# A two-layer hybrid encoder on one core: one late tile in three outputs, softmax scalings on another engine, ten matmuls ahead of the first

## The chip, the cores and the metric

The kernel runs on one core of a Trainium2 chip. Its time is the device time of one execution in microseconds; three runs of the kernel before gave 2385.94, 2385.95 and 2386.65 us, median 2385.95. A core has five engines with queues of their own: PE (TensorE, matrix products into PSUM), DVE (VectorE), ACT (ScalarE), POOL (GpSimd) and SP (SyncE, which here issues every transfer). They are ordered among each other by semaphores alone.

## The reference

Two layers of the following, on `x` of 512 tokens by 1024 channels, in float32:

```python
x = x + 0.5 * swiglu(rmsnorm(x, ffn1_norm[l]), ffn1_w1[l], ffn1_w2[l])
h = rmsnorm(x, mix_norm[l])
q, k, v, xr, yr, gl = jnp.split(h @ w_in[l], SPLITS, axis=-1)
# 16 query heads, 4 key heads of 64: per-head rmsnorm, rotary, softmax over all 512 keys
attn = block_attention(q, k, v) @ w_attn_o[l]
# depthwise conv of xr, two gated linear recurrences (forward, backward), times gelu(yr)
rnn = (hr * jax.nn.gelu(yr)) @ w_rnn_o[l]
merged = gates[:, :, 0] * attn + gates[:, :, 1] * rnn      # sigmoid gates from gl
x = x + merged @ w_out[l]
x = x + 0.5 * swiglu(rmsnorm(x, ffn2_norm[l]), ffn2_w1[l], ffn2_w2[l])
```

## The kernel before

Activations lie channel-major: a tile is 128 channels by 512 tokens, and `x` is 8 such tiles. Every float32 product is made of three matmuls on PE (`mm3`, L233): operands are split in a high and a low part, and high x high, high x low and low x high are accumulated in PSUM. `run` (L238) makes one output tile of 128 channels from 8 (or 22, or 4) input tiles that way. Weights come as one ordered stream of chunks of four tiles; SP loads them nine chunks ahead, and ACT (`wh`) and DVE (`wl`) split them six chunks ahead.

The order of all other work is tied to the matmul stream. Behind every second input tile `run` calls `step()`. Work is queued with `later(n, fn)` and issued n steps on; what an engine gets in which order follows from that alone, and each engine works its queue strictly in that order.

A layer is: first FFN half; the mixing phase; second FFN half. In the mixing phase the input projections of the recurrent branch and of the gates run on PE, and the attention and the recurrence run beside them as side work. Attention is made in 64 units over both layers (a head and half of the queries, two tiles of 128 queries each). For a unit, PE makes the scores (`u_sc`, L635), DVE their row maxima (`u_max`, L639) and from both the negated, scaled bias for the exponential (L641), ACT the exponential `p` with row sums, DVE the reciprocal of the sums (L649) and that times 2^14 (L650), POOL the high half of the probabilities (`pH`, by L114), DVE their low half (by L108). Then they are transposed by a transfer, and PE multiplies them with the values (L684). The names `un` are the small tiles of a unit: maxima, bias, sums, reciprocals.

The recurrence uses `xc` (the convolution), `tr` and `ti` (its gates, and then its terms), `y` (the gelu). POOL has `ti` (L111) and one step of `y` (L114) of it.

At the end of the phase stand three projections: `rnn`; `aoa` and `ao` (the first and the second four input tiles of the attention's output projection); and `wo`, the output projection of the phase, whose eight input tiles are the merged tiles `mg`. Evacuating an output m of `ao` (`ev_ao`, L885) makes, on DVE, the attention's part `aa` and the gated `th`, adds the recurrent part (on POOL, for the last output on DVE), and then splits the sum into `mh` (ACT) and `ml` (DVE):

Of the kernel before, what the change touches and what calls it, by code (L numbers as in the profile page):

```python
# [9 lines left out]
F32R = mybir.dt.float32r  # L10
# [8 lines left out]
KD = D // 128  # L19
# [10 lines left out]

GELU_K = 0.7978845608028654

# k tiles per weight chunk, 2 KB slots of the pool, chunks loaded and split ahead
KC = 4

NT = 99
LOAD_AHEAD = 9
SPLIT_AHEAD = 6

# side work, in steps of six matmuls of the main stream: lags of its stages, where the  # L40
# gate chunks go, and heads started per step
PV_LAG = 6
N_LAGS = (4, 2)
G_LAGS = (1, 2, 3, 5, 7)
# [4 lines left out]
GATES_3 = 1  # L49
GATES_4 = 0  # L50
AO_AT = 4
Q1_AT = 0
RATES = {"kv": 0.0, "q": 0.33, "xr": 0.33, "gA": 0.33, "gB": 0.33, "yr": 0.33, "lru0": 0.3, "lru1": 0.3, "rnn": 0.6, "aoa": 0.6, "ao": 0.0, "wo": 0.0}

# [2 lines left out]
def tile_griffin_encoder(  # L57
# [55 lines left out]
    def gts(out, a, s1, s2, op0=ALU.mult, op1=ALU.mult):  # L113
        G.tensor_scalar(out=out, in0=a, scalar1=s1, scalar2=s2, op0=op0, op1=op1)  # L114
# [1 line left out]
    def f32(ap):  # L116
        return ap.bitcast(F32)

    # ---- steps: side work is queued against the progress of the main matmul stream
    pend = []  # L120
    clock = [0, 0]
    launcher = []
# [5 lines left out]
    def step():  # L128
        clock[0] += 1
        while pend and pend[0][0] <= clock[0]:  # L130
            heapq.heappop(pend)[2]()
        for f in launcher:
            f()
# [2 lines left out]
        while pend:  # L136
            step()

    # ---- weights: one ordered stream of chunks, loaded ahead and split ahead
    chunks = []  # L140

    KS = {"aoa": (0, KD // 2), "ao": (KD // 2, KD)}
# [81 lines left out]
    def next_w():  # L224
        i = pos[2]
        pos[2] += 1
        load_to(i + 1)
        split_to(i + 1)
        load_to(i + 1 + LOAD_AHEAD)
        split_to(i + 1 + SPLIT_AHEAD)  # L230
        return split.pop(i)

    def mm3(ps, wh, wl, xh, xl, start, stop):  # L233
        PE.matmul(ps, wh, xh, start=start, stop=False)  # L234
        PE.matmul(ps, wh, xl, start=False, stop=False)  # L235
        PE.matmul(ps, wl, xh, start=False, stop=stop)  # L236
# [8 lines left out]
            if k % 2 == 1:  # L245
                step()

    # ---- constants
    ones = const.tile([128, 128], F32R, name="ones")
    idn = const.tile([128, 128], F32, name="idn")  # L250
    tabs = const.tile([128, 2, 4, HD], F32, name="tabs")
# [10 lines left out]
        prm_t[l] = t  # L262

    class Norm:
        """h = x * gain in two parts per tile, and the sum of squares over the tiles."""

        def __init__(self, l, col):
            self.l, self.col = l, col
# [46 lines left out]
                V.tensor_reduce(out=rtok, in_=d3, op=ALU.add, axis=AX)  # L315
            return r, rtok

    # ---- SwiGLU half step: x += 0.5 * (silu(h @ w1g) * (h @ w1u)) @ w2
    def ffn(norm, on_x, during=None, r_at=0):
        h = norm.h  # L320
        at = [None] * KF
# [58 lines left out]
            else:  # L380
                fin()

    # ---- per-layer vectors for the mixing phase
    def layer_vectors(l):
        p = prm_t[l]
        v = {}
# [50 lines left out]
        v["tb"] = tb  # L437
        return v

    # ---- mixing phase  # L440
    def mix(l, norm, v, on_x):
        p = prm_t[l]
        hb, hc, nhc, sc, tb = v["hb"], v["hc"], v["nhc"], v["sc"], v["tb"]
# [26 lines left out]
        vs = {}  # L470
        ready = [0]

        # heads of q or k: per-head norm, rotary, two fp16 parts, transposed
        def heads(src, n, cs, stack_h, stack_l, dst_T):
            st = {}

# [131 lines left out]
            for t in range(4):  # L608
                later(8 + t, lambda t=t: v3(t))

        # attention: (pair of heads, half of the queries, head, query tile)
        units = [(pp, hf, hi) for pp in range(NH // 2) for hf in range(2) for hi in range(2)]
        attn = [None] * KD
        up = [0, 0.0, 0.0]
# [9 lines left out]
        def unit(pp, hf, hi):  # L624
            head, kv = 2 * pp + hi, pp // 2
            mx, nb, su, ri, rs = (sm("un", 2) for _ in range(5))
            ps, pe = [None, None], [None, None]
            src = []

            def u_sc(ti):  # L630
                ps[ti] = PS()
                q = qT[head // 8, 2 * hf + ti]
                for kt in range(4):
                    for j in range(2):
                        PE.matmul(ps[ti][:, kt * 128:(kt + 1) * 128], q[:, head % 8, :], kT[kt][:, 2 * kv + j, :],  # L635
                                  start=j == 0, stop=j == 1)

            def u_max(ti):
                V.tensor_reduce(out=mx[:, ti:ti + 1], in_=ps[ti], op=ALU.max, axis=AX)  # L639
                if ti == 1:  # L640
                    V.tensor_scalar(out=nb, in0=mx, scalar1=sc, scalar2=-1.0, op0=ALU.mult, op1=ALU.mult)  # L641

            def u_exp(ti):
                pe[ti] = T("p")
                act(pe[ti], ps[ti], ACTF.Exp, bias=nb[:, ti:ti + 1], scale=sc, accum_out=su[:, ti:ti + 1])

            def u_inv(ti):
                if ti == 0:
                    V.reciprocal(ri, su)  # L649
                    V.tensor_scalar(out=rs, in0=ri, scalar1=2.0 ** 14, scalar2=None, op0=ALU.mult)  # L650

            def u_hi(ti):
                if ti == 0:
                    src.extend(T("pH", F16, (128, 2, 512)) for _ in range(2))
                gts(src[0][:, ti], pe[ti], ri[:, ti:ti + 1], 2.0 ** 14)

            def u_lo(ti):
                stt(src[1][:, ti], pe[ti], rs[:, ti:ti + 1], src[0][:, ti], ALU.mult, ALU.subtract)

            def u_tr():  # L660
                dst = [T("PT", F16, (128, 2, 4, 128)) for _ in range(2)]
                for i in range(2):
                    SP.dma_start_transpose(dst[i].rearrange("p a b c -> p (a b) c"),
                                           src[i].rearrange("p a b -> p (a b)"))
                pts[pp, hf, hi] = dst

            u_sc(0)
            later(1, lambda: u_sc(1))
            for n, f in zip(U_LAGS, (u_max, u_exp, u_inv, u_hi, u_lo)):
                for ti in range(2):  # L670
                    later(n + ti, lambda f=f, ti=ti: f(ti))
            later(U_LAGS[5], u_tr)
            if hi == 1:
                later(U_LAGS[5] + PV_LAG, lambda: pv(pp, hf))
# [24 lines left out]

        launcher.append(launch)  # L700

        # q, k, v: token-major
        def qkv_chunk(ps, k, src):
            wh, wl = next_w()
            hh, hl = src[k]
# [28 lines left out]
                heads([q[:] for q in q_t], 8, tb["q"], stack_h(qview), stack_l(qview),  # L734
                      lambda t, s_: trans_q(i, t, s_))

        # recurrent branch
        rnn = [None] * KD
        rst = {}

# [115 lines left out]
            for n, f in zip(G_LAGS, (e1, e2, e3, e4, e5)):  # L856
                later(n, f)

        # gates and output projections
        th = {}  # L860
        tm = [None] * KD
        mg = [None] * KD
# [53 lines left out]
        for op, m in mix_ops:  # L916
            up[2] = RATES[op]
            if op[:3] == "lru":
                lru(m, int(op[3]))
                continue  # L920
            if op in ("kv", "q"):
                qkv(op, m)
                continue
            if m == 0 and op in ("rnn", "ao"):
                while pend and (rst if op == "rnn" else True):
                    if op == "ao":
                        up[2] = 1.0
                    step()
                for k in range(2):
                    fetch(1 if op == "rnn" else 0, k)  # L930
            if op == "ao" and m == 0:
                launcher.pop()
            if op == "wo" and m == 0:
                for k in range(KD):
                    x[k] = T("x")
                    SP.dma_start(out=x[k], in_=xsave[k])
            if op in ("rnn", "ao"):
                fetch(1 if op == "rnn" else 0, m + 2)
            ps = PS()
            run(ps, {"rnn": rnn, "aoa": attn, "ao": attn, "wo": mg}.get(op, hn), *KS.get(op, (0, KD)))  # L940
            if m == KD - 1 and op in ("ao", "wo"):
                evac[op](m, ps)
            else:
                later(1, lambda op=op, m=m, ps=ps: evac[op](m, ps))

    with tc.manual_schedule():
        V.memset(f32(ones), 1.0)
        V.memset(epsb, EPS)
        warm = const.tile([128, 1], F32, name="warm")
        act(warm, epsb, ACTF.Tanh)  # L950
        load_prm(0)
        for k in range(KD):
            x[k] = T("x")
        norm = Norm(0, P_G1)
        for k in range(KD):
            SP.dma_start(out=x[k], in_=xT[k])
            if k in (0, 3, 6):
                load_to(pos[0] + 1)
        load_to(5)
        for k in range(KD):  # L960
            norm.add_h(k)
            if k in (0, 3, 7):
                split_to(pos[1] + 1)
        split_to(4)
        for k in range(KD):
            later(1 + k, lambda k=k: norm.add_sq(k))
        later(18, norm.close)
        later(30, lambda: SP.dma_start(out=tabs, in_=rope))
        later(30, lambda: SP.dma_start(out=idn, in_=ident))

        for l in range(L):
            nmix = Norm(l, P_GM)
            vecs = {}
            ffn(norm, nmix.add, lambda: vecs.update(layer_vectors(l)), 0 if l else 2)
            nf = Norm(l, P_G2)
            if l + 1 < L:
                load_prm(l + 1)
            mix(l, nmix, vecs, nf.add)
            if l + 1 < L:
                norm = Norm(l + 1, P_G1)  # L980
                ffn(nf, norm.add)
            else:
                ffn(nf, lambda m: SP.dma_start(out=outT[m], in_=x[m]))
        drain()
# [68 lines left out]
```

## Time and profile before

| | |
|---|---|
| median of three runs | 2385.95 us |
| span of the profiled execution (first to last instruction) | 2385.1 us |
| mean granted TensorE clock, share of 2.4 GHz | 0.997 |
| PE busy | 2359.3 us, 99%, 11604 matmuls |
| DVE busy | 1519.6 us, 64% |
| ACT busy | 1035.8 us, 43% |
| POOL busy | 263.1 us, 11%, 236 instructions |
| chain that ended last | PE 90%, DVE 5%, ACT 3%, DMA 1% |

The profiled execution has no time of its own beside its span; the runs' median lies 0.85 us above the span. Busy time of PE is modelled and its matmuls overlap, so its share is not a measure of speed; what counts is when the next matmul starts and what it waited for. The busy shares are means over stages with different limits: DVE, 64% in the mean, is over 90% busy in those twelve of the forty equal slices of the span that hold the mixing phase's middle. An instruction's row shows its start in us from the first instruction, its length in us, and in brackets the idle time of its engine before it with what ended that.

### The profile page before, as it was taken

How to read it: one execution, taken by the hardware profiler on the slowest of the kernel's cores; microseconds unless marked ns; L12 is line 12 of the kernel's file. 1: busy time of each engine (PE TensorE's matmuls, PEld its weight loads, DVE VectorE, ACT ScalarE, POOL GpSimd, SP SyncE). 2: the span in 40 equal slices, each digit the busy share in tenths (PEclk: the TensorE clock that was granted, in tenths of full speed). 3: DMA queues.
4: the chain of work that ended last, by engine and by line, in shares of the span. 5: the costliest groups of instructions: out<-in, count | busy, mean ns of one | idle time of the engine just before them, and what ended most of it. 6: DMA issues, size and time to landing. Idle time of an engine off the chain costs nothing.

```text
span 2385.1 us, 31932 instructions
## 1 busy us (share of the span) xinstructions
PE 2359.3 (99%) x11604; PEld 1927.3 (81%) x11604; DVE 1519.6 (64%) x2520; ACT 1035.8 (43%) x1892; POOL 263.1 (11%) x236
## 2 busy tenths in 40 slices
PE   8999999999999999999999999999999999999999
PEld 7888888877778788888888888888787787888887
DVE  6555536899995755553355555378999966655521
ACT  5333324678863333232233333256788533333321
POOL 1000000122331200000000000001223312000000
PEclk9999999999999999999999999999999999999999
DMA  5222333676488232223332223336665972222331
GB/s 202 97 86 85 102 98 110 155 157 150 118 206 240 89 98 88 88 84 111 109 103 89 84 85 110 107 94 157 158 149 124 209 231 95 97 85 85 93 98 66
DMA packets 299486, 285.83 MB, mean 120 GB/s; under 512 B 175936, under 2 KB 184512, under 8 KB 299328
## 3 DMA queue, kind: packets, MB, share of 16 engines
q1 hardware_dynamic: 299328, 283.79, 42.4%
q8 instruction: 91, 1.49, 0.3%
q14 instruction: 67, 0.55, 0.1%
HBM read 229.18 MB, written 14.68 MB: 102 GB/s over the span
## 4 chain that ended last, share of the span: by engine, by line
PE 90%; DVE 5%; ACT 3%; DMA 1%; issue 1%; SPq 0%; DVEq 0%; ACTq 0%
PE ps L234 27%; PE ps L235 27%; PE ps L236 27%; PE ps L708 2%; PE ps L635 2%; PE ps L710 2%; PE ps L709 2%; PE ps L684 1%; DVE wl L105 1%; DVE pH L108 1%; DVE tr L108 0%; ACT p L102 0%; DVE un L639 0%; DMA x<-in_xT_dram 0%; ACT L102 0%
## 5 line engine op out<-in xcount | busy, mean ns | idle before, releaser
L105 DVE TENSOR_TENSOR wl<-wr,wh 128x512 fp32r<-128x512 f32 (+1 forms) x848 | 580.5, 717 | 69.9 <-ACT wh L102 68.5
L234 PE MATMUL ps<-hh,wh 128*128 128x512 f32 x1408 | 549.0, 390 | 6.2 <-ACT wh L102 5.7
L235 PE MATMUL ps<-hl,wh 128*128 128x512 f32 x1408 | 548.7, 390 | 0.2 <-DVE hl L108 0.2
L236 PE MATMUL ps<-hh,wl 128*128 128x512 f32 x1408 | 548.5, 390 | 0.0
L102 ACT ACTIVATE wh<-wr 128x512 fp32r<-128x512 f32 (+1 forms) x848 | 477.2, 602 | 80.4 <-DMA wr<-in_w2b_dram 68.5
L234 PEld LDWEIGHTS ps<-hh,wh 128*128 128x128 f32 x1408 | 264.8, 188 | 61.9 <-ACT wh L102 5.7
L235 PEld LDWEIGHTS ps<-hl,wh 128*128 128x128 f32 x1408 | 264.8, 188 | 56.3 <-DVE hl L108 1.3
L236 PEld LDWEIGHTS ps<-hh,wl 128*128 128x128 f32 x1408 | 264.7, 188 | 54.8 <-DVE wl L105 0.2
L234 PE MATMUL ps<-ah,wh 128*128 128x512 f32 x704 | 273.9, 389 | 0.0
L235 PE MATMUL ps<-al,wh 128*128 128x512 f32 x704 | 273.9, 389 | 0.0
L236 PE MATMUL ps<-ah,wl 128*128 128x512 f32 x704 | 273.9, 389 | 0.0
L102 ACT ACTIVATE ah<-u 128x512 fp32r<-128x512 f32 x88 | 55.7, 633 | 376.5 <-DVE u L105 376.5
L234 PE MATMUL ps<-hnh,wh 128*128 128x512 f32 x512 | 207.8, 406 | 6.6 <-ACT tr L102 5.4
L108 DVE SCALAR_TENSOR_TENSOR x<-ps,x 128x512 f32<-128x512 f32 x48 | 33.2, 691 | 271.3 <-PE ps L236 271.3
L236 PE MATMUL ps<-hnh,wl 128*128 128x512 f32 x512 | 201.0, 393 | 0.0
L235 PE MATMUL ps<-hnl,wh 128*128 128x512 f32 x512 | 200.2, 391 | 0.0
L111 POOL TENSOR_TENSOR sq<-sq,sq 128x512 f32<-128x512 f32 x42 | 56.7, 1350 | 1132.4 <-ACT sq L102 1118.3
L102 ACT ACTIVATE hh<-x,prm 128x512 fp32r<-128x512 f32 x48 | 34.5, 723 | 314.8 <-DVE x L108 310.4
L105 DVE TENSOR_TENSOR u<-ps,R 128x512 f32<-128x512 f32 x88 | 60.8, 691 | 168.7 <-PE ps L236 168.7
L102 ACT ACTIVATE th<-g 128x512 f32<-128x512 f32 x88 | 55.6, 632 | 245.7 <-DVE g L105 245.7
L114 POOL TENSOR_SCALAR pH<-p,un 128x512 f16<-128x512 f32 x128 | 115.6, 913 | 351.3 <-DVE un L649 197.9
L234 PEld LDWEIGHTS ps<-ah,wh 128*128 128x128 f32 x704 | 132.1, 188 | 27.5
(157 smaller groups left out, 3465.7 us busy)
## 6 DMA issues: line engine op xcount, KB each, us to landing
wr<-in_w1a_dram SPq DMA_DIRECT2D x176, 256.0 KB, 2.7
wr<-in_w1b_dram SPq DMA_DIRECT2D x176, 256.0 KB, 2.7
wr<-in_wfm_dram SPq DMA_DIRECT2D x128, 256.0 KB, 3.3
wr<-in_w2a_dram SPq DMA_DIRECT2D x80, 256.0 KB, 2.7
wr<-in_w2b_dram SPq DMA_DIRECT2D x80, 256.0 KB, 2.8
wr<-in_wqkv_dram SPq DMA_DIRECT2D x48, 256.0 KB, 2.9
gsave<-lg SPq DMA_DIRECT2D x32, 256.0 KB, 3.3
wr<-in_wro_dram SPq DMA_DIRECT2D x32, 256.0 KB, 3.9
```

Of the source, the lines that this page charges most:

```text
L102: A.activation(out, in_, func, **kw)
L105: V.tensor_tensor(out=out, in0=a, in1=b, op=op)
L108: V.scalar_tensor_tensor(out=out, in0=a, scalar=s, in1=b, op0=op0, op1=op1)
L111: G.tensor_tensor(out=out, in0=a, in1=b, op=op)
L114: G.tensor_scalar(out=out, in0=a, scalar1=s1, scalar2=s2, op0=op0, op1=op1)
L234: PE.matmul(ps, wh, xh, start=start, stop=False)
L235: PE.matmul(ps, wh, xl, start=False, stop=False)
L236: PE.matmul(ps, wl, xh, start=False, stop=stop)
L635: PE.matmul(ps[ti][:, kt * 128:(kt + 1) * 128], q[:, head % 8, :], kT[kt][:, 2 * kv + j, :], start=j == 0, stop=j == 1)
L708: PE.matmul(ps[t], hh[:, ts_], wh, start=k == 0, stop=False)
L709: PE.matmul(ps[t], hh[:, ts_], wl, start=False, stop=False)
L710: PE.matmul(ps[t], hl[:, ts_], wh, start=False, stop=k == KD - 1)
```

## The change

It has three parts.

- In `wo`, the first three outputs are made by a new function, `run_open`: it makes input tiles one to seven of the first output, then of the second, then of the third, leaving all three accumulations open in PSUM, and after that the eighth input tile of each of the three. Their evacuations are issued one, two and three steps later. The other five outputs are made by `run` as before.
- In a unit's softmax, DVE's maximum gives the negated maximum, and its scaling to the bias goes to POOL, one instruction for each query tile behind its maximum. The scaling of the reciprocal by 2^14 goes to POOL too, and the high half takes the scaled reciprocal.
- Ahead of everything, POOL sets a tile to ones and PE makes ten matmuls of it.

```diff
+    def run_open(pss, rhs, kl):
+        held = []
+        for ps in pss:
+            for k in range(kl):
+                if k % KC == 0:
+                    wh, wl = next_w()
+                sl = slice(k % KC * 128, (k % KC + 1) * 128)
+                mm3(ps, wh[:, sl], wl[:, sl], *rhs[k], k == 0, False)
+                if k % 2 == 1:
+                    step()
+            held.append((wh, wl))
+        sl = slice(kl % KC * 128, (kl % KC + 1) * 128)
+        for ps, (wh, wl) in zip(pss, held):
+            mm3(ps, wh[:, sl], wl[:, sl], *rhs[kl], False, True)
+            yield ps
...
             def u_max(ti):
-                V.tensor_reduce(out=mx[:, ti:ti + 1], in_=ps[ti], op=ALU.max, axis=AX)
-                if ti == 1:
-                    V.tensor_scalar(out=nb, in0=mx, scalar1=sc, scalar2=-1.0, op0=ALU.mult, op1=ALU.mult)
+                V.tensor_reduce(out=mx[:, ti:ti + 1], in_=ps[ti], op=ALU.max, axis=AX, negate=True)
+                gts(nb[:, ti:ti + 1], mx[:, ti:ti + 1], sc, 1.0)
...
                     V.reciprocal(ri, su)
-                    V.tensor_scalar(out=rs, in0=ri, scalar1=2.0 ** 14, scalar2=None, op0=ALU.mult)
+                    gts(rs, ri, 2.0 ** 14, 1.0)
...
-                gts(src[0][:, ti], pe[ti], ri[:, ti:ti + 1], 2.0 ** 14)
+                gts(src[0][:, ti], pe[ti], rs[:, ti:ti + 1], 1.0)
...
                     SP.dma_start(out=x[k], in_=xsave[k])
+                for i, ps in enumerate(run_open([PS() for _ in range(WO_OPEN)], mg, KD - 1)):
+                    later(1 + i, lambda m=i, ps=ps: evac["wo"](m, ps))
+                continue
+            if op == "wo" and m < WO_OPEN:
+                continue
...
+        idle = T("idle", F32R)
+        G.memset(f32(idle), 1.0)
+        pw = PS()
+        for _ in range(WARM):
+            PE.matmul(pw, idle[:, 0:128], idle, start=True, stop=True)
```

`WO_OPEN` is 3, `WARM` is 10, `gts` is a `tensor_scalar` on POOL. On the engines the change looks as follows; tile numbers differ between the two kernels, and line numbers by two.

PE in the first layer's `wo`, before: the end of the first output, with input tile seven (`mh_8147`) and input tile eight (`mh_8159`), and the begin of the second (`ps_8218`).

```order
L236 MATMUL ps_8179<-mh_8121,wl_8026 128x512
L234 MATMUL ps_8179<-mh_8147,wh_8025 128x512
L235 MATMUL ps_8179<-ml_8148,wh_8025 128x512
L236 MATMUL ps_8179<-mh_8147,wl_8026 128x512
L234 MATMUL ps_8179<-mh_8159,wh_8025 128x512
L235 MATMUL ps_8179<-ml_8160,wh_8025 128x512
L236 MATMUL ps_8179<-mh_8159,wl_8026 128x512
L234 MATMUL ps_8218<-mh_7984,wh_8053 128x512
L235 MATMUL ps_8218<-ml_7985,wh_8053 128x512
```

PE in the changed kernel at the same place: input tile seven is `mh_8192`, and behind it the second output (`ps_8225`) begins.

```order
L236 MATMUL ps_8224<-mh_8192,wh_8070 128x512
L237 MATMUL ps_8224<-ml_8193,wh_8070 128x512
L238 MATMUL ps_8224<-mh_8192,wl_8071 128x512
L236 MATMUL ps_8225<-mh_8029,wh_8098 128x512
L237 MATMUL ps_8225<-ml_8030,wh_8098 128x512
```

Farther on, at the end of the third output's seven tiles, input tile eight (`mh_8204`) comes for all three.

```order
L236 MATMUL ps_8226<-mh_8192,wh_8178 128x512
L237 MATMUL ps_8226<-ml_8193,wh_8178 128x512
L238 MATMUL ps_8226<-mh_8192,wl_8179 128x512
L236 MATMUL ps_8224<-mh_8204,wh_8070 128x512
L237 MATMUL ps_8224<-ml_8205,wh_8070 128x512
L238 MATMUL ps_8224<-mh_8204,wl_8071 128x512
L236 MATMUL ps_8225<-mh_8204,wh_8126 128x512
L237 MATMUL ps_8225<-ml_8205,wh_8126 128x512
L238 MATMUL ps_8225<-mh_8204,wl_8127 128x512
```

So the matmuls of input tile eight moved behind 42 others, and those of tile seven kept their place in the first output.

ACT at the end of the first layer's `ao`, before: the high halves of merged tiles six, eight (`mh_8159`) and seven (`mh_8147`), with weight splits between.

```order
L102 ACTIVATE mh_8121<-th_8020 128x512
L102 ACTIVATE mh_8159<-th_8076 128x512
L102 ACTIVATE wh_8182<-wr_8079 128x512
L102 ACTIVATE mh_8147<-th_8048 128x512
L102 ACTIVATE wh_8202<-wr_8105 128x512
```

ACT in the changed kernel at the same place, where tile eight is `mh_8204` and tile seven `mh_8192`.

```order
L104 ACTIVATE mh_8166<-th_8065 128x512
L104 ACTIVATE mh_8204<-th_8121 128x512
L104 ACTIVATE wh_8229<-wr_8124 128x512
L104 ACTIVATE mh_8192<-th_8093 128x512
L104 ACTIVATE wh_8249<-wr_8150 128x512
```

Nothing moved here.

POOL in the first layer's attention, before: one unit's two `pH` and the recurrence's `ti` and gelu's `y` around them.

```order
L111 TENSOR_TENSOR ti_5830<-ti_5830,tr_5828 128x512
L114 TENSOR_SCALAR pH_6086<-p_5954,un_5863 128x512
L114 TENSOR_SCALAR pH_6086<-p_5972,un_5863 128x512
L111 TENSOR_TENSOR ti_6021<-ti_6021,tr_6019 128x512
L114 TENSOR_SCALAR y_6142<-y_6142 128x512
L114 TENSOR_SCALAR pH_6204<-p_6122,un_5979 128x512
```

POOL in the changed kernel at the same place: `un` with `scs` is the scaling of a maximum to the bias, `un` from `un` alone that of the reciprocals.

```order
L113 TENSOR_TENSOR ti_5858<-ti_5858,tr_5856 128x512
L116 TENSOR_SCALAR un_5892<-un_5891 128x2
L116 TENSOR_SCALAR un_6006<-un_6005,scs_2277 128x1 x2
L116 TENSOR_SCALAR pH_6116<-p_5983,un_5892 128x512
L116 TENSOR_SCALAR pH_6116<-p_6001,un_5892 128x512
L116 TENSOR_SCALAR un_6009<-un_6008 128x2
L113 TENSOR_TENSOR ti_6051<-ti_6051,tr_6049 128x512
L116 TENSOR_SCALAR y_6172<-y_6172 128x512
L116 TENSOR_SCALAR un_6184<-un_6183,scs_2277 128x1
L116 TENSOR_SCALAR pH_6235<-p_6152,un_6009 128x512
```

A unit's `pH` now stand behind the scaling of its reciprocals and behind the next unit's two biases, which wait for that unit's maxima.

## Rows read from the trace of the kernel before

**Rows 1.** Waits of PE, whole execution: waiter <- releaser: us in total, times, longest

```profile
PE ps L234 <- ACT mh L102: 6.8, 2, 3.4
PE ps L234 <- ACT tr L102: 5.4, 2, 2.7
PE ps L234 <- ACT p L102: 1.4, 4, 0.5
```

**Rows 2.** Timeline of PE, first layer's wo: start, length, engine, line, operation, count, [idle]

```profile
785.55 0.39 PE L234 MATMUL ps<-mh,wh 128*128 128x512 f32 x1
...
788.95 0.39 PE L234 MATMUL ps<-mh,wh 128*128 128x512 f32 x1
...
793.74 0.79 PE L234 MATMUL ps<-mh,wh 128*128 128x512 f32 x1 [3.38 <-ACT mh L102]
...
795.65 0.63 PE L234 MATMUL ps<-mh,wh 128*128 128x512 f32 x1
...
800.31 0.40 PE L234 MATMUL ps<-mh,wh 128*128 128x512 f32 x1
```

**Rows 3.** Timeline of ACT, same stretch

```profile
792.02 0.63 ACT L102 ACTIVATE mh<-th 128x512 fp32r<-128x512 f32 x1 [4.26 <-DVE th L105]
...
793.08 0.61 ACT L102 ACTIVATE mh<-th 128x512 fp32r<-128x512 f32 x1
```

**Rows 4.** Chain of waits, 600 to 640 us: start, us on the chain, what

```profile
618.43 0.07 DVE un L641
...
618.56 0.69 DVE ti L108
...
624.41 0.74 DVE pH L108
...
626.52 0.07 DVE un L650
...
626.60 0.69 DVE tr L108
...
630.19 0.61 DVE y L105
...
632.08 0.50 PE ps L234
...
635.95 0.27 PE ps L234
```

**Rows 5.** Groups by line and shape: xcount | busy us, mean ns | idle before

```profile
L114 POOL TENSOR_SCALAR pH<-p,un 128x512 f16<-128x512 f32 x128 | 115.6, 913 | 351.3 <-DVE un L649 197.9 <-ACT wh L102 39.2 <-issue 25.6
...
L641 DVE TENSOR_SCALAR un<-un,scs 128x2 f32<-128x2 f32 x64 | 22.6, 354 | 2.3
...
L1042 POOL MEMSET const-float32-0.0<- 128x1 f32 x1 | 0.1, 98 | 0.2 <-issue 0.2
```

**Rows 6.** Timeline of all engines, 603.5 to 608.5 us

```profile
605.93 0.23 DVE L641 TENSOR_SCALAR un<-un,scs 128x2 f32<-128x2 f32 x1
...
606.67 0.68 DVE L108 SCALAR_TENSOR_TENSOR tr<-a,tr 128x512 f32<-128x512 f32 x1
...
607.44 1.67 POOL L111 TENSOR_TENSOR ti<-ti,tr 128x512 f32<-128x512 f32 x1 [1.59 <-DVE tr L108]
...
607.87 1.78 DVE L108 SCALAR_TENSOR_TENSOR tr<-a,tr 128x512 f32<-128x512 f32 x1
```

**Rows 7.** Timeline of POOL, 612 to 616 us

```profile
613.44 1.36 POOL L114 TENSOR_SCALAR pH<-p,un 128x512 f16<-128x512 f32 x2 [1.61 <-DVE un L649]
```

**Rows 8.** Timeline of all engines, 5 to 15 us

```profile
5.67 0.80 PE L234 MATMUL ps<-hh,wh 128*128 128x512 f32 x1 [5.67 <-ACT wh L102]
...
7.85 0.80 PE L234 MATMUL ps<-hh,wh 128*128 128x512 f32 x1 [0.54 <-ACT hh L102]
...
13.63 0.75 DVE L108 SCALAR_TENSOR_TENSOR hl<-x,prm,hh 128x512 fp32r<-128x512 f32 x1 [0.58 <-ACT hh L102]
...
14.44 0.50 PE L235 MATMUL ps<-hl,wh 128*128 128x512 f32 x1 [0.17 <-DVE hl L108]
```

More of the change, by code (lines that the diff above doesn't have):

```diff
@@ L36 @@
 NT = 99
+WARM = 10
 LOAD_AHEAD = 9
@@ L51 @@
 AO_AT = 4
+WO_OPEN = 3
 Q1_AT = 0
```

## The prediction

> **What bounds the kernel now.** I read the page first: PE is busy for 2359.3 of 2385.1 us, and 90% of the chain that ended last is PE. So the time can only move where PE waits, or where its clock is at the lower of its two levels. The list of who waited for whom, for PE alone over the whole execution, has its largest entries in three places [rows 1]: `mh` from ScalarE (6.8 us, two times), `tr` from ScalarE (5.4 us, two times), and `p` (1.4 us, four times). The first belongs to the start of `wo`, the second and third to the attention stage. In the FFN halves, most of the span, PE waits for nothing but the very first weights. Each of the three parts of the change touches one such place, so I take them in turn.
>
> The profiled execution has a span of 2385.1 us; the runs' median is 2385.95, 0.85 more. I sum against 2385.1 and add 0.85 at the end. Less than about 0.2%, 4.8 us, cannot be told from no change here.
>
> **Part 1, the late eighth tile.** An output of `wo` is 8 tiles of three matmuls. In the timeline of PE at the first output [rows 2] the matmul at 785.55 is the first and the one at 788.95 the sixteenth, so a matmul takes 3.40/15 = 0.227 us. The stall ends at 793.74. The rows between let one count which tile this is: it is the nineteenth matmul, so three times six stand ahead of it, and it opens the **seventh** tile. The eighth starts at 795.65 and waits for nothing. The 34th matmul starts at 800.31; 33 steps should take 7.5 us and took 14.8. So 7.3 us go in this layer, partly to the stall, partly to the lower clock behind it (steps of 0.43 us, the 1.2 GHz level), and with the same stall in the second layer at most 14.6 us are to be had.
>
> Why the seventh? For the last output of `ao` the halves `hi` and `lo` are issued at once (L907), for the one before they are queued for two and three steps later (L904), and those steps come only inside `wo`. So ScalarE makes tile eight's half at 792.02 and tile seven's at 793.08 [rows 3], and the order lists show that order before and after. The changed kernel holds back tile eight alone: the three matmuls with the seventh tile still stand seventh in the first open output. PE reaches them at the same moment, waits until the same 793.7, and finds only then 42 matmuls that it could have done. The steps, the weight splits and the evacuation of `ao` stand in the same order on VectorE and ScalarE until there. I cost this part at nothing: 0 us, with bounds 0 and -14.6. Behind the stall, the three evacuations come one step apart instead of four; PE does not read `x` until the FFN. The three late tiles use weights that are already split, so they wait for nothing.
>
> **Part 2, the softmax scalings.** Per unit (a head, half the queries; 64 in all) VectorE loses two small instructions, the negated scaling of the maxima (L641) and the scaling of the reciprocal (L650). Their mean durations overstate the gain, for neighbours overlap; in the chain of waits, where VectorE is the chain, the next instruction starts 0.13 us behind one and 0.08 us behind the other [rows 4]: 0.21 us a unit. The mean of L641 is 0.354 us, a usual one 0.23 [rows 5, 6]: the rest, 0.12, is time in which it was held up, which goes with it. Saved: 0.33 us a unit.
>
> Added are three small instructions a unit on GpSimd. None like them stands in the trace. Nearest from below is a constant's memset of 128x1, 0.098 us; nearest from above a scaling of 128x512, `pH`, of which two take 1.36 us undisturbed, 0.68 each, and 0.913 in the mean [rows 5, 7]. On VectorE 512 columns take 0.68 us as well, and the small L641 0.23, so the size is worth some 0.45; I take 0.2 us, nearer to the memset.
>
> What they cost elsewhere is the open question. At 607.44 GpSimd begins `ti`, 1.67 us; the `tr` that VectorE starts at 607.87, two operands in SBUF, takes 1.78 where the one before took 0.68 [rows 6]. The two engines shut each other out. If half of the new instructions hold VectorE up for their 0.2 us, a unit loses 3 x 0.5 x 0.2 = 0.3 us, and 0.33 was saved: the two cancel. The Trainium skill, "SBUF — State Buffer", "Who interferes with whom", has a rule that speaks against this part: a GpSimd instruction that reads SBUF takes an exclusive lock on a port pair, and a VectorE instruction with two inputs in SBUF blocks until it ends, and the other way round. The pair at 607 agrees; taken to the letter, each new instruction blocks such a neighbour for its length, and the sum would be the third rival's below.
>
> The new instructions also form waits in GpSimd's queue: the pair of `pH` that starts at 613.44 [rows 7] now stands behind two scalings that wait for the next unit's maxima, which VectorE ends at about 618.4, where L641 starts. Its reader on VectorE comes at 624.41 [rows 4]; 618.4 + 0.4 + 1.4 = 620.2, so 4 us of cover are left. ScalarE's exponentials gain on one side: the first no longer waits for the second maximum.
>
> What is the relief worth? The `tr` stall ends at 632.08 with VectorE's `y` at 630.19 just ahead in the chain [rows 4], and VectorE has some 2.5 units' small instructions in the 30 us before. At 0.03 us a unit that is 0.1 us a layer, 0.2 in all. Bounds: if VectorE's lag went altogether, `tr` and `p` would vanish, 6.8 us, and the lower clock that follows in the first layer: ten matmuls' starts from 632.08 to 635.95 span 3.87 us instead of 9 x 0.227 = 2.04, so 1.8 more, -8.6. If each new instruction cost VectorE a full 0.68: 2.04 - 0.33 = 1.7 us a unit, 4.3 a layer, +8.6. I take -0.2.
>
> **Part 3, the ten matmuls of ones.** They need only a memset, so they can run while PE waits for its first weights until 5.67 [rows 8]. In before, the first matmuls run at the lower level. From 5.67 to the 23rd matmul at 14.44 pass 8.8 us, and 22 steps at 0.227 would be 5.0, so 3.8 us seem to be on offer. But the 23rd waits for data: the eighth tile of `x` has its low half at 13.63 + 0.75 = 14.38, and PE had run ahead to it with a wait of 0.17 us. A faster PE waits there longer. All inputs are there from then on. The cost: ten matmuls at 0.43 us are 4.3 us, and the three of the first tile that stand behind them 1.3; the second tile's data hold PE until 7.85 anyhow. So nothing is lost if the memset is done by 7.85 - 5.6 = 2.2 us, and one of 0.1 to 0.9 us [rows 5], near the start, should be. So 0 us, between -3.8 and +1.8 (a lower clock behind 14.44, priced as after 632).
>
> **Sum.** 0 - 0.2 + 0 = -0.2: a span of 2384.9, a time of 2385.7 us.
>
> **Rivals.**
> - *The stall at `wo` goes.* For it: the change is built for a late tile, and 14.6 us lie there. Against: the late tile is the seventh. Time 2385.95 - 14.6 = 2371.3. Chance 0.04.
> - *VectorE's relief empties its queue.* It is over 90% busy in the slices of this stage, and a queue near saturation answers strongly. Against: the saving is 0.33 us before any new hold-up, and GpSimd takes some back. Time 2385.95 - 8.6 = 2377.4. Chance 0.14.
> - *GpSimd's small instructions hold up VectorE* (this ends on the other side). With 0.4 us each and every one in the way, a unit loses 1.2 - 0.33 = 0.87 us, 2.2 a layer ahead of the `tr` stall, 4.4 in all, and the second layer's stall, longer, brings the lower clock too, 1.8: 2385.95 + 6.2 = 2392.2. It decides from 0.33 us of hold-up a unit; VectorE's high share in the stage speaks for it, the short memset against it. Chance 0.13.
> - *The forecast*: nothing to tell. Chance 0.69.
>
> The forecast's own range is 2382 to 2389. The fast relief and the slow hold-up both reach into the range below in part; 2378 to 2391 leaves out about 2 in 10. Faster by over 0.2%: 0.04 + 0.14 = 0.18; slower: 0.13; within: 0.69.
>
> **What would show it.** Part 1: in both layers PE's wait for `mh` is still there, about 3.4 us, at the nineteenth matmul of `wo`, and ScalarE's two `mh` are still in that order. If it is gone or at the matmul 64th in line, this step is wrong. Part 2: VectorE has 128 instructions less and its two `tr` waits on PE stand within 1 us of 2.7; GpSimd's small groups have a mean near 0.2 us; a mean of 0.4 or more with longer VectorE neighbours is the third rival, a wait under 1 us the second. Part 3: the granted clock is at its upper level sooner, and the 23rd real matmul still starts at about 14.4. A change of more than 4.8 us proves me wrong.

## The result, and the profile after

| | before | after |
|---|---|---|
| time, median of four runs each | 2386.01 us | 2399.14 us |
| ratio, 95% interval | | 1.0055 (1.004 to 1.0069) |
| span of the profiled execution | 2385.1 us | 2396.2 us |
| first FFN matmul | 5.67 us | 6.19 us |
| first matmul of the second FFN half, layer 1 | 836.36 us | 841.00 us |
| first matmul of the second FFN half, layer 2 | 2021.49 us | 2032.69 us |

The changed kernel is slower by 13.1 us; forecast was 2385.7, between 2378 and 2391. The profiled execution took 2398.01 us. The last three lines of the table, read from PE's timeline, place the loss. PE's first matmul starts 0.5 us later than before, but the 23rd starts 0.95 us earlier (13.49 against 14.44 [rows 8]), and that lead is kept to the first mixing phase. At its end PE is 4.6 us behind, so the phase loses 5.6 us; the second loses 6.6, and the FFN halves behind the first matmuls lose nothing. The mean granted clock is 0.997 in both profiled executions, so the 11.1 us between their spans are not time at a lower clock level.

The changed kernel's page begins with the busy time of each engine:

```profile
PE 2362.9 (99%) x11614; PEld 1929.1 (81%) x11614; DVE 1508.2 (63%) x2392; ACT 1037.1 (43%) x1892; POOL 401.8 (17%) x429
```

DVE has 128 instructions less and POOL 193 more: 192 scalings and a memset. POOL's busy time has grown by 138.7 us, though the new instructions work on one or two columns each. The waits of PE, whole execution (waiter <- releaser: us in total, times, longest), answer to [rows 1]:

```profile
PE ps L236 <- ACT tr L104: 7.3, 4, 2.1
PE ps L236 <- ACT mh L104: 6.8, 2, 3.4
PE ps L655 <- DVE xc L110: 4.5, 4, 1.5
PE ps L236 <- DVE xc L110: 4.5, 2, 2.3
PE ps L236 <- DVE oL L110: 1.5, 2, 0.8
```

The wait for `mh` has not moved by a tenth. `tr` has grown from 5.4 us to 7.3 and comes four times instead of twice; the waits for `xc` are nearly new (0.5 us before). These belong to the attention stage, where the recurrence's side work runs beside the softmax.

**At `wo`.** PE's timeline of the changed kernel at the stall (start, length, engine, line, operation, count, [idle]):

```profile
799.18 0.49 PE L236 MATMUL ps<-mh,wh 128*128 128x512 f32 x1 [3.38 <-ACT mh L104]
```

and ACT's in the same stretch:

```profile
797.46 0.63 ACT L104 ACTIVATE mh<-th 128x512 fp32r<-128x512 f32 x1 [4.26 <-DVE th L107]
...
798.52 0.61 ACT L104 ACTIVATE mh<-th 128x512 fp32r<-128x512 f32 x1
```

Against [rows 2, 3] everything stands 5.4 us later: `wo` begins at 790.99, and its nineteenth matmul waits the same 3.38 us for the second of the two `mh`, tile seven's. Only the stretch of slow steps behind the stall ends 0.8 us sooner, which is why the FFN half behind it starts 4.6 us late and not 5.4; the kernel with the scalings alone, whose `wo` is that of before, shows 0.9 us of the same.

**At the start.** PE's timeline, which answers to [rows 8]:

```profile
1.31 4.24 PE L977 MATMUL ps<-idle 128*128 128x512 f32 x10 [1.31 <-POOL idle L974]
...
6.19 0.50 PE L236 MATMUL ps<-hh,wh 128*128 128x512 f32 x1 [0.64 <-ACT wh L104]
...
13.49 0.50 PE L237 MATMUL ps<-hl,wh 128*128 128x512 f32 x1 [0.29 <-DVE hl L110]
```

The ten matmuls end before the weights are there, and the real ones run at the upper clock level early (0.23 us apart from 8.26 on; before, from 11.33 on). Then they wait for `hl` as before. That the 23rd starts at 13.49 is not their doing: in the kernel with the reciprocals alone (below), which has no such matmuls, it starts at 13.23.

**In the attention stage.** The groups of POOL (xcount | busy us, mean ns | idle before), next to [rows 5]:

```profile
L116 POOL TENSOR_SCALAR pH<-p,un 128x512 f16<-128x512 f32 x128 | 122.3, 962 | 0.9
L116 POOL TENSOR_SCALAR un<-un,scs 128x1 f32<-128x1 f32 x128 | 115.7, 904 | 120.1 <-DVE un L659 109.2 <-ACT wh L104 6.4 <-PE ps L655 2.4
...
L116 POOL TENSOR_SCALAR un<-un 128x2 f32<-128x2 f32 x64 | 20.6, 321 | 162.4 <-DVE un L668 162.4
```

The shortest of the 192 takes 0.185 us, the shortest bias 0.26, the longest 4.65; the mean of a bias is 904 ns for 128 numbers, nearly what a `pH` of 512 columns takes. And POOL now stands 109.2 us before a bias, waiting for DVE's maximum (L659). What that does is seen in the timelines of one stretch, next to [rows 6, 7]. POOL first:

```profile
608.52 0.64 POOL L116 TENSOR_SCALAR un<-un,scs 128x1 f32<-128x1 f32 x1 [0.40 <-DVE un L659]
609.72 2.44 POOL L116 TENSOR_SCALAR un<-un,scs 128x1 f32<-128x1 f32 x1 [0.56 <-ACT wh L104]
612.14 1.35 POOL L116 TENSOR_SCALAR pH<-p,un 128x512 f16<-128x512 f32 x2
613.46 1.73 POOL L113 TENSOR_TENSOR ti<-ti,tr 128x512 f32<-128x512 f32 x1
615.28 0.62 POOL L116 TENSOR_SCALAR y<-y 128x512 f32<-128x512 f32 x1
```

DVE beside it:

```profile
608.95 0.67 DVE L659 TENSOR_REDUCE un<-ps 128x1 f32<-128x512 f32 x1
609.55 0.67 DVE L107 TENSOR_TENSOR rl<-tr,rh 128x512 fp32r<-128x512 f32 x1
610.15 0.67 DVE L110 SCALAR_TENSOR_TENSOR tr<-a,tr 128x512 f32<-128x512 f32 x1
610.76 0.68 DVE L107 TENSOR_TENSOR wl<-wr,wh 128x512 fp32r<-128x512 f32 x1
611.36 0.68 DVE L110 SCALAR_TENSOR_TENSOR tr<-a,tr 128x512 f32<-128x512 f32 x1
...
615.93 0.69 DVE L107 TENSOR_TENSOR y<-y,ps 128x512 f32<-128x512 f32 x1 [1.90 <-POOL y L116]
```

And ACT and PE:

```profile
616.65 0.63 ACT L104 ACTIVATE y<-y 128x512 f32<-128x512 f32 x1 [2.61 <-DVE y L107]
617.19 0.67 ACT L104 ACTIVATE tr<-ps,hb 128x512 f32<-128x512 f32 x1
```
```profile
617.91 0.50 PE L236 MATMUL ps<-hnh,wh 128*128 128x512 f32 x1 [2.10 <-ACT tr L104]
```

Before, POOL's `y` and its reader on DVE stood so:

```profile
609.20 0.94 POOL L114 TENSOR_SCALAR y<-y 128x512 f32<-128x512 f32 x1
```
```profile
610.60 0.68 DVE L105 TENSOR_TENSOR y<-y,ps 128x512 f32<-128x512 f32 x1
```

Read the rows of the changed kernel from the top: the second bias cannot start before its maximum, DVE's of 608.95, which ends at 609.62 (the row of the bias names a weight split of ACT that ended at about the same moment). DVE then runs four instructions with two operands in SBUF, and POOL's bias ends only when the last of them does, at about 612.1. `pH`, `ti` and `y` stand behind it in POOL's queue. From the end of the second maximum to the start of `y` it is 5.7 us; before it was 3.3, from L641 at 605.93 [rows 6] to 609.20. The bias's 2.44 us, against 0.26 for the shortest, are most of that difference of 2.4: in this stretch the wait brings POOL to the start of DVE's run, and the run holds it there. DVE waits 1.90 us for `y`, ACT 2.61 for DVE, and `tr`, which stands behind `y` in ACT's queue, comes too late for PE. The chain of waits of the same kernel (start, us on the chain, what), which answers to [rows 4], runs through the same rows:

```profile
609.74 0.09 POOL un L116
...
612.14 1.35 POOL pH L116 x2
613.49 1.69 POOL ti L113
...
615.28 0.63 POOL y L116
...
615.93 0.70 DVE y L107
...
616.65 0.63 ACT y L104
617.28 0.58 ACT tr L104
```

Over the whole execution, the waits of DVE, and then of ACT, on this path:

```profile
DVE y L107 <- POOL y L116: 23.1, 12, 2.8
DVE pH L110 <- POOL pH L116: 8.8, 14, 0.8
```
```profile
ACT p L104 <- POOL un L116: 32.5, 20, 5.2
ACT y L104 <- DVE y L107: 13.8, 10, 2.6
```

Before, DVE did not wait for `pH` at all, and the other three were:

```profile
DVE y L105 <- POOL y L114: 1.0, 2, 0.5
```
```profile
ACT p L102 <- DVE un L641: 19.3, 11, 3.0
ACT y L102 <- DVE y L105: 8.4, 6, 1.6
```

### The profile page after: what moved, and what is told of

It reads as the page before. It is cut to its first block, busy times and chain, and to the rows that moved or that the text cites. A ratio compares the mean times of both kernels' runs of the same rounds, so it can differ in the third digit from the quotient of the medians.

```text
span 2396.2 us, 32005 instructions
## 1 busy us (share of the span) xinstructions
PE 2362.9 (99%) x11614; PEld 1929.1 (81%) x11614; DVE 1508.2 (63%) x2392; ACT 1037.1 (43%) x1892; POOL 401.8 (17%) x429
## 4 chain that ended last, share of the span: by engine, by line
PE 83%; DVE 7%; issue 3%; ACT 3%; POOL 2%; DMA 1%; SPq 0%; POOLq 0%; DVEq 0%; ACTq 0%
PE ps L236 25%; PE ps L237 25%; PE ps L238 25%; PE ps L727 2%; PE ps L729 2%; PE ps L728 2%; DVE wl L107 1%; DVE pH L110 1%; PE ps L655 1%; POOL un L116 1%; PE ps L703 1%; DVE tr L832 1%; DVE un L659 1%; DVE xc L110 1%; ACT tr L104 1%
## 5 line engine op out<-in xcount | busy, mean ns | idle before, releaser
L107 DVE TENSOR_TENSOR wl<-wr,wh 128x512 fp32r<-128x512 f32 (+1 forms) x848 | 590.5, 730 | 68.2 <-ACT wh L104 66.8
L238 PEld LDWEIGHTS ps<-ah,wl 128*128 128x128 f32 x704 | 132.2, 188 | 27.5
L237 PEld LDWEIGHTS ps<-al,wh 128*128 128x128 f32 x704 | 132.2, 188 | 27.4
```

What stands on the lines that cost most here:

```text
L107: V.tensor_tensor(out=out, in0=a, in1=b, op=op)
```

## The experiments

All are timed against the kernel before, which gave 2386.0 to 2386.1 us in each group.

**The changed kernel with its scalings put back.** Parts 1 and 3 without part 2.

```diff
-V.tensor_reduce(..., op=ALU.max, axis=AX, negate=True)
-gts(nb[:, ti:ti + 1], mx[:, ti:ti + 1], sc, 1.0)
+V.tensor_reduce(..., op=ALU.max, axis=AX)
+if ti == 1:
+    V.tensor_scalar(out=nb, in0=mx, scalar1=sc, scalar2=-1.0, ...)
...
-gts(rs, ri, 2.0 ** 14, 1.0)
+V.tensor_scalar(out=rs, in0=ri, scalar1=2.0 ** 14, ...)
```

> The changed kernel with the softmax scalings put back on VectorE; the open outputs and the ten matmuls stay. Theory (the scalings on GpSimd are the whole loss, 13 us): 2385 to 2386, equal to before within 1.5 us, since PE's wait for `mh` (3.4 us, twice) is untouched by the open outputs and the start waits for data. Rival (the open outputs, their late evacuations or the ten matmuls lose too): 2390 or more.

Measured: 2385.79 us, ratio 1.0 (0.999 to 1.0009); PE waits 6.8 us for `mh`. Parts 1 and 3 cost nothing and gain nothing that can be told.

**The kernel before with the scalings alone**, and of those the bias alone, and the reciprocals alone. The edit is the diff of part 2, or its first or its second half.

> The kernel before with the three small scalings of a unit moved to GpSimd and nothing else. Theory: 2398 to 2400, the whole loss. Rival: under 2394.

> The kernel before with only the bias moved to GpSimd (two instructions a unit), the reciprocal's scaling stays on VectorE. Theory (a bias starts behind a maximum while VectorE has runs of instructions with two inputs in SBUF, is shut out for 0.4 to 4 us, and what is queued behind it is late): nearly all of the loss, 2395 to 2399. Rival (each small instruction on GpSimd costs the same, two thirds of them are here): 2394 to 2395, and the next kernel the other third.

> The kernel before with only the reciprocal's scaling moved to GpSimd (one instruction a unit). Theory: it was shut out seldom (51 of 64 took 0.19 us), so 2385 to 2387, no loss. Rival (a price for each): 2390.

Measured: 2400.47 us (ratio 1.0061, 1.0046 to 1.0076), 2400.94 (1.0063, 1.0048 to 1.0078) and 2389.69 (1.0015, 1.0005 to 1.0024). Part 2 is the whole loss, 14.4 us, and the bias alone makes it; that the changed kernel lost 13.1 lies within the intervals. The reciprocals cost 3.6 us by themselves: not the theory's nothing, but the 2390 of the rival. On top of the bias they cost nothing, so the two don't add, and a price for each instruction doesn't fit either.

**The bias on ScalarE**, in the queue of the exponential that reads it.

```diff
-gts(nb[:, ti:ti + 1], mx[:, ti:ti + 1], sc, 1.0)
+act(nb[:, ti:ti + 1], mx[:, ti:ti + 1], ACTF.Copy, scale=sc)
```

> The scalings alone, with the bias on ScalarE instead of GpSimd (the reciprocal's scaling stays on GpSimd). Theory: no lock-out there, the biases wait only for ScalarE's own queue, 128 x some 0.2 us = 26 us more on an engine that is 85% busy in the stage: 2385 to 2392. Rival (any hop of the bias to another engine costs 14 us): 2397 or more.

Measured: 2466.56 us, ratio 1.0338 (1.0321 to 1.0355): a miss by 75 us. The waits of ACT name it:

```profile
ACT un L102 <- DVE un L639: 190.6, 118, 4.3
```

The 128 instructions take 37.6 us of work, 294 ns each, without any lock-out by DVE; but 118 times ACT stands still before one, and ACT has the weight splits and the recurrence's gates behind it. The mean granted clock of this execution is 0.984, against 0.997 before, so up to some 30 of the 80 us (an estimate: 0.016 of 2463 us less 0.003 of 2385) are PE's lower clock level behind its new waits. That the price of the hand-over grew with what the queue holds behind it is my reading; no run varied that alone.

**A bias that only writes.** POOL writes a constant over the maximum, 128x1, and so still has to wait for DVE's maximum, but reads nothing.

```diff
-gts(nb[:, ti:ti + 1], mx[:, ti:ti + 1], sc, 1.0)
+G.memset(mx[:, ti:ti + 1], -1.0)
...
-act(pe[ti], ps[ti], ACTF.Exp, bias=nb[:, ti:ti + 1], scale=sc, ...)
+act(pe[ti], ps[ti], ACTF.Exp, bias=mx[:, ti:ti + 1], scale=1e-12, ...)
```

> The scalings alone on GpSimd as in the run of that name, but the bias is written by a memset to a constant over the maximum, which still waits for the maximum; the exponential takes that constant and a constant scale (so the softmax is not computed). Same places and same waits in GpSimd's queue, same latency to the exponential, only nothing is read. Theory (a bias scaling reads SBUF and is shut out while VectorE runs instructions with two inputs there): the memsets take 0.1 us each and most of the 14.4 us goes, 2386 to 2390. Rival (the wait for the maximum in GpSimd's queue, or the extra hop to the exponential, is the loss): 2396 to 2400.

Measured: 2396.66 us, ratio 1.0044 (1.0029 to 1.0059). The theory as I had put it, that shutting the bias itself out of SBUF is the price, falls: the memsets are not shut out and 10.6 of 14.4 us stay. POOL's timeline shows that, and also that the lock-out is not gone, so that 3.8 us is not its price:

```profile
608.73 0.10 POOL L640 MEMSET un<- 128x1 f32 x1 [1.10 <-DVE un L639]
608.85 3.45 POOL L114 TENSOR_SCALAR pH<-p,un 128x512 f16<-128x512 f32 x2
612.27 1.71 POOL L111 TENSOR_TENSOR ti<-ti,tr 128x512 f32<-128x512 f32 x1
614.07 0.62 POOL L114 TENSOR_SCALAR y<-y 128x512 f32<-128x512 f32 x1
```

The memset ends in 0.10 us, but the two `pH` that waited behind it now start into the same run of DVE's instructions, and take 3.45 us where two took 1.36 undisturbed [rows 7]. The lock-out has moved from the bias to the `pH`: over the whole execution their mean is 1297 ns, with the scalings 965. So this run does not show what the wait costs without the lock-out.

**Without `y` in POOL's queue.** The gelu's constant goes into the scale of ScalarE's square, its addition into DVE's next instruction; once with the scalings, once without them.

```diff
-act(y2, ps, ACTF.Square)
-gts(y2, y2, 0.044715, 1.0, ALU.mult, ALU.add)
-tt(y2, y2, ps, ALU.mult)
+act(y2, ps, ACTF.Square, scale=0.044715 ** 0.5)
+stt(y2, y2, 1.0, ps, ALU.add, ALU.mult)
```

> The scalings alone on GpSimd, and the gelu's step y on GpSimd taken away: the constant goes into ScalarE's square, the + 1 into VectorE's product (same number of instructions there). Theory: the loss reaches PE by VectorE's wait for y (22 us in 12 waits) more than by the exponentials; with that link gone about half or more of the 14.4 us is back: 2388 to 2393. Rival (the way is by the exponentials or pH): 2397 or more.

> The control: the kernel before with the gelu's step on GpSimd taken away in the same manner, scalings on VectorE as before. Theory: before, y on GpSimd was late by nothing that the chain shows, so 2384 to 2387, no change; what the run before this one gains beyond that is the link.

Measured: 2389.14 us with the scalings (ratio 1.0011, 1.0002 to 1.0021), 2383.39 without (0.9988, 0.9979 to 0.9998). The scalings cost 5.75 us when `y` isn't behind them and 14.4 when it is: 8.6 us of the loss go with `y`. PE's waits agree in part. With `y` taken away, those for `tr` are 4.6 us with the scalings and 4.7 without them, so that part is gone; those for `xc`, 9.0 us in the run of the scalings alone, are still 4.9, and the exponentials still wait 30.9 us for POOL.

**The bias queued later.** Issued three steps behind its maximum and one ahead of the exponential; the reciprocals stay on VectorE.

```diff
-                gts(nb[:, ti:ti + 1], mx[:, ti:ti + 1], sc, 1.0)
+            def u_bias(ti):
+                gts(nb[:, ti:ti + 1], mx[:, ti:ti + 1], sc, 1.0)
...
+            for ti in range(2):
+                later(U_LAGS[1] - 1 + ti, lambda ti=ti: u_bias(ti))
```

> The kernel before with the 128 bias scalings on GpSimd as in the changed kernel (reciprocal scaling left on VectorE), but each issued three steps after its maximum, one step ahead of the exponential, where the changed kernel issues it in the same step as the maximum. With the bias in the maximum's step the loss was 14.8 us. Theory (GpSimd's queue stands still at its head because the bias is queued before its maximum exists, and y stands behind it): the maximum is mostly there when GpSimd comes to the bias, GpSimd's wait for VectorE's maxima falls from some 110 us to under 30, and at least 10 of the 14.8 us come back: 2386 to 2391 us. Rival (the instructions themselves are the price, shut out by VectorE's two-input instructions or holding them up, wherever they stand): 2396 to 2401 us.

Measured: 2395.43 us, ratio 1.0039 (1.0024 to 1.0054): below what the rival said and well above what the theory said. POOL's wait for the maxima fell to 62.0 us (286.7 with the bias alone), not under 30. The waits of DVE, and then of ACT, show where the rest is:

```profile
DVE y L105 <- POOL y L114: 3.1, 6, 0.5
```
```profile
ACT p L102 <- POOL un L114: 53.0, 31, 3.7
```

The way through `y` is closed (21.7 us with the bias alone), but the exponentials now wait 53.0 us for POOL (23.8 there): the bias stands behind `ti` and `y` instead of before them. Later helps one queue and harms the next. That left two readings, the waits or the instruction itself.

**The instruction by itself, and with the wait alone.** 128 more instructions of the bias's form on POOL, into a tile that nobody reads, DVE's own scalings left as they are; once from a constant, once from the maximum.

```diff
 V.tensor_reduce(out=mx[:, ti:ti + 1], in_=ps[ti], op=ALU.max, axis=AX)
+gts(dum[:, ti:ti + 1], sc, sc, 1.0)                 # first kernel
+gts(dum[:, ti:ti + 1], mx[:, ti:ti + 1], sc, 1.0)   # second kernel
```

> The kernel before with 128 extra instructions on GpSimd, one behind each maximum's step, of the bias's form (128x1 by a scalar per partition) but from a constant into a tile that nobody reads: they wait for nothing and nobody waits for them; VectorE's own scalings stay. What the instruction itself costs, with no wait in either direction. Theory (the loss of 14.8 us is made of waits: GpSimd's queue standing behind the maxima, and ScalarE's behind the bias): 2386 to 2389 us. Rival (the price is the instruction and the engines shutting each other out): 2395 to 2401 us, the 9.4 us that were left when the bias was queued later.

> The same 128 extra instructions, but each reads the maximum of its step, so that GpSimd's queue waits for VectorE as with the bias; nobody reads the result, the exponentials take VectorE's bias as before. What the wait in GpSimd's queue costs without the hand-over to ScalarE. Theory: GpSimd waits some 250 to 300 us for the maxima, VectorE's y waits about 20 us for GpSimd's y, and 8 to 12 of the 14.8 us are there: 2394 to 2398 us; what is missing to 2400.9 is the exponentials' wait for GpSimd. Rival (the hand-over to ScalarE is the greater part): 2387 to 2391 us.

Measured: from a constant 2386.77 us, ratio 1.0003 (0.9994 to 1.0013); from the maximum 2410.73, ratio 1.0102 (1.0087 to 1.0117). POOL's group in the first kernel:

```profile
L114 POOL TENSOR_SCALAR dum<-scs 128x1 f32<-128x1 f32 x128 | 69.9, 558 | 0.7
```

These too are shut out by DVE: mean 558 ns, shortest 260, longest 1294. They cost the kernel nothing that can be told. In the second kernel POOL waits for the maxima and DVE for `y`:

```profile
POOL dum L114 <- DVE un L640: 286.3, 109, 10.2
```
```profile
DVE y L105 <- POOL y L114: 17.7, 12, 2.7
```

There 24.7 us are lost, twice the most that I had expected. So it is the wait for the maximum that turns 128 harmless instructions into a loss, and no hand-over to the exponentials is needed for it. It is not shown that the wait does it without the lock-out: behind its maximum the same instruction takes 825 ns in the mean, not 558, and VectorE's `pH` 904, not 825. That this kernel loses more than the bias alone (14.8) leaves two differences, not tried apart: VectorE keeps its 64 scalings, and the first exponential still waits for the second maximum. Its granted clock is also lower, 0.993 against 0.996.

**Two late tiles at `wo`.** The first three outputs hold back tile seven and tile eight, in the kernel before; and then this together with the gelu's step taken from POOL.

```diff
+    def run_open(pss, rhs, kl, late=1):
...
+            for k in range(kl, kl + late):
+                sl = slice(k % KC * 128, (k % KC + 1) * 128)
+                mm3(ps, wh[:, sl], wl[:, sl], *rhs[k], False, k == kl + late - 1)
...
+                for i, ps in enumerate(run_open([PS() for _ in range(WO_OPEN)], mg, KD - 2, 2)):
```

> The kernel before, with the first three outputs of wo left open with their last two input tiles late (the seventh and the eighth), and nothing else changed. Theory (the stall of part 1 sits at the seventh tile, so holding back the eighth alone could not reach it): the two waits of PE for mh (6.8 us) and most of the lower-clock stretch behind them go, 13 to 14.6 us in all: 2371 to 2373 us. Rival (the stall is only put off, because the halves come as late as VectorE and ScalarE have work, or PE meets another wait later in wo): 2380 to 2386 us.

> The two edits that lower the time, together: three outputs of wo open with two late tiles, and the gelu step y of GpSimd taken into ScalarE's square and VectorE's next step, with the softmax scalings as before. If the two add up: the time of two late tiles alone less 2.7 us, so 2368 to 2370 us. Rival (the later start of the work in wo takes back what the attention stage gains): no better than two late tiles alone, 2371 to 2373 us.

Measured: 2373.41 us, ratio 0.9947 (0.9932 to 0.9962); together 2369.86, ratio 0.9933 (0.9917 to 0.995). The waits of PE in the first of them no longer hold `mh` at all:

```profile
PE ps L235 <- ACT wh L103: 6.3, 1, 6.3
PE ps L235 <- ACT tr L103: 5.4, 2, 2.7
PE ps L235 <- ACT p L103: 1.4, 4, 0.5
PE ps L236 <- DVE ml L106: 0.6, 2, 0.3
```

The two gains add up, and 2369.86 us beats both kernels: 16.2 us under the kernel before, 29.3 under the changed one.

## Why the prediction was wrong

- **Part 1, 0 us: right.** The stall sits at tile seven, as the order lists said; holding back tile eight alone moved nothing. Of the 14.6 us said to lie there, holding back both gave 12.7.
- **Part 3, 0 us: right.** The ten matmuls end in time, the early matmuls run at the upper level, and PE meets the last tile of `x` anyway. The sign given for it, the 23rd matmul at about 14.4, did not come (13.49), but it comes as early without the ten matmuls. The kernel with parts 1 and 3 alone takes the time of before.
- **Part 2, the size of the instructions: right undisturbed** (0.185 us for the reciprocals, 0.26 for a bias, against 0.2 taken), **and wrong in the trace** (904 ns), because VectorE holds them up. The other direction was overrated: VectorE's busy time fell by 11.4 us, where 0.33 x 64 = 21 were to be saved, so by this difference 0.15 us a unit came back as hold-up, and 0.3 was said. That GpSimd's small instructions are held up is by itself nothing that PE feels: those from a constant, held up as well, cost nothing.
- **Part 2, the step that failed:** "The new instructions also form waits in GpSimd's queue", which ended with "so 4 us of cover are left". The step saw that a bias waits for the next unit's maxima and followed one reader, that of `pH`, in one unit; over the whole execution even that reader came to wait, 14 times. Behind `pH` in the same queue stand `ti` and `y`, as the order rows under the change show, and `y` had hardly any cover: in the rows of before it ended at 610.14 and its reader started at 610.60, 0.46 us later. The step also took 0.4 us for the two biases behind their maxima. But the end of a maximum is where a run of VectorE's two-operand instructions can begin, and in the stretch shown one bias alone took 2.44 us. That delay went on to PE's waits for `tr` and, through DVE, to some of the new ones for `xc`. The kernels with a waiting and a waitless extra instruction, 24.7 us and 0.7, show the wait to be what makes the loss; how much of it is the lock-out that follows the wait, no run separates. The pair with and without `y` shows 8.6 of the 14.4 us to go with `y`. How the other 5.75 divide among `pH`, `ti`, the exponentials and VectorE's own hold-up, I did not try.
- **The third rival** had the direction, and its sign came: a mean over 0.4 us, and longer neighbours on VectorE (its `pH` 916 ns, 817 before). But its hold-up of VectorE was to give 2392.2, and it is hardly the greater part of the loss: without `y` on GpSimd VectorE's `pH` are held up as well, 959 ns in the mean, and 5.75 us are lost. It was priced at 0.13 because VectorE's hold-up was the only slow mechanism considered. Of the second rival, the relief of VectorE, no run shows anything by itself; the share of over 90% that it leans on stands in eight slices of the page of before, not in twelve.

On the lock-out itself, the Trainium skill ("SBUF — State Buffer", "Who interferes with whom") says that an instruction with two SBUF inputs on VectorE contends with one on GpSimd that reads SBUF and not with one that only writes it. The memsets of 0.10 us beside such instructions and the biases of up to 4.65 agree. What it costs by itself, no run here shows. The Trainium skill ("PSUM — Partial Sum Buffer", section "Engine vs sequencer instructions") calls the queues of ScalarE, VectorE and GpSimd strictly first in, first out; the 118 stops of ScalarE and the 109 of GpSimd agree; the prediction's step on the queue needed that rule followed to the queue's end.

## What to carry to other kernels

Moving a tiny instruction to an idle engine moves its wait too: in a queue worked in order, what stands behind a waiting instruction waits with it, so list every instruction behind it up to the next idle time and look up the cover of each, not of the nearest alone. Look too at what the other engine does at the moment when the wait ends: here it was often a run of instructions that shut the new one out. An engine that is busy 11% of the time can be critical if one of its instructions has no slack, and then it must not wait for anything late. And before work is put aside for a late operand, count the matmuls to the stall: it names the operand that is late.

## What the runs showed of the hardware

- Beside four VectorE instructions with two SBUF operands, back to back, one 128x1 instruction of GpSimd, 0.26 us at its shortest, took 2.44 us, and the longest, at 482.35 beside eight, took 4.65: GpSimd did not get in between them. It can: at 607.44 of the kernel before [rows 6] `ti` did, and VectorE's next `tr` took 1.78 us. A memset of 128x1 behind the maximum takes 0.098 us.
- 128 instructions of 128 numbers, moved to ScalarE, took 294 ns each, 37.6 us in all. The kernel lost 80 us, with 118 stops of ScalarE before them and a mean granted clock of 0.984.
- The first matmuls ran at the upper clock level from 8.26 us on behind ten matmuls of ones, from 11.33 on without them, and the kernel was no faster.
